# Gate silus placed behind the last exponential of the decays in a hybrid convolution and state-space layer

## The chip, the cores and the metric

The kernel runs on one core of a Trainium2 chip. The metric is the device time of one execution in microseconds. Before the change the median of three runs is 1958.61 us (1958.3 to 1961.29).

The engines are named as in the profile: PE is TensorE (matmuls), DVE is VectorE, ACT is ScalarE, POOL is GpSimd, SP is SyncE, which here only issues DMAs. Each engine takes its instructions in the order in which they stand in its own queue, and waits in that order.

## The reference

One layer mixes a convolution branch and a Mamba-2 (SSD) branch, and a gated MLP with a short convolution follows. 1024 positions, width 1024. What matters here is the SSD branch, in chunks of 128 positions, 4 groups of 8 heads:

```python
a_cs = jnp.cumsum(a, axis=-1)
seg = a_cs[..., :, None] - a_cs[..., None, :]
decay = jnp.where(causal, jnp.exp(jnp.where(causal, seg, 0.0)), 0.0)
cb = jnp.einsum("bclgn,bcsgn->bcgls", cc, bc)
y_diag = jnp.einsum("bcgrls,bcsgrp->bclgrp", cb[:, :, :, None] * decay, xs)
...
yg = (y.reshape(bsz, t, SSM_DIM) * jax.nn.silu(z.astype(jnp.float32)))
```

`decay` needs an exponential, and `silu(z)` is the gate with which the branch's output is multiplied. `z` is a part of the input projection `h @ w_in`.

## The kernel before

The sequence is done in two halves of 512 positions (`hh` 0 and 1), each by `mixers(hh, hT)`. Every fp32 matrix is split in a high and a low part and a product takes three matmuls (`mm3`, L183 to L185), so that a column block of 128 channels (`column`) costs PE 24 matmuls of 128x512. Its result lies in one of four PSUM banks (`acc`), which are used in turn: a bank comes free when another engine has read the result. `col_weights` loads a block's weights by DMA, ACT makes the high part (L149) and, in half 0, DVE the low part (L154).

`mixers` goes through four groups. For each one it makes the column blocks of B, C and four of x, with a convolution of four taps (`conv4`: u on ACT, L417 to L419, taps on DVE, L421, a silu on ACT, L431); then the four gate blocks (`z_gate`, a silu on ACT at L483 straight out of PSUM into `zs`); then two blocks for the long convolution (`glu`, with a sigmoid, L442); then the SSD itself (`ssd_group`); then the 31 taps of the long convolution (`conv31`, L466), on DVE at the lowest priority.

`ssd_group` runs over the group's four chunks. Per chunk: `ab` (the cumulated sums, spread over the partitions by a DMA from SP, L506); eight Relus into `m` (L519) and one exponential over `m` (L526); an exponential `ce` (L529), which POOL multiplies with C (L530); the masked product of `m` (L546) on DVE; matmuls with `m` and `ce` on PE (L551, L554); the state (L559 to L566); the gate product (L579). `m`, `ab` and `ce` have one buffer each, so that the Relus of a chunk wait until PE has used up the `m` of the chunk in front of it.

The order in which instructions stand on the engines is set by a scheduler of the build, which estimates times and goes by priorities. A manual dependency (`issue_after`) orders two instructions of the same engine without a wait. The scheduler lets the column blocks of one group run among the SSD chunks of the group in front of it: so the gate silus of group g stand on ACT among the Relus and exponentials of the last chunk of group g - 1. ACT holds one table of functions at a time; where a silu follows an exponential, or the other way round, the build puts an ACT_TABLE_LOAD between them.

Of the kernel before, what the change touches and what calls it, by code (L numbers as in the profile page):

```python
# [10 lines left out]
AF = mybir.ActivationFunctionType  # L11
# [39 lines left out]
CT_A, CT_G, CT_X, CT_B, CT_C, CT_GA, CT_GB, CT_Z = 0, 8, 16, 32, 36, 40, 48, 56  # L51
# [4 lines left out]
def kernel(  # L56
# [16 lines left out]
    V, A, G, TE, SY = nc.vector, nc.scalar, nc.gpsimd, nc.tensor, nc.sync  # L73
# [14 lines left out]
    def bank(which):  # L88
        n_ps[0] += 1
        pl, tag = (pacc, "acc") if which else (psm, "sm")  # L90
        return pl.tile([P, 512], F32, tag=tag, name=f"{tag}{n_ps[0]}")
# [17 lines left out]
        out=quads, in_=ident.rearrange("p (j h) -> p h j", j=4), axis=AX.X, op=ALU.add  # L109
# [29 lines left out]
    }  # L139
    y_scr = [dram.tile([8, P, HALF], F32, name=f"y_scr{i}") for i in range(2)]  # L140

    casts, los = [], []

    def weights(src, name, keep=None, kept=None):
        with tc.high_priority(offset=4000):
# [16 lines left out]
    def col_weights(hh, ct):  # L162
        scr = low_scr.get(ct)
        return weights(
            wcol[ct], f"c{hh}_{ct}", None if hh else scr, scr if hh else None
        )

    def issue_after(later, earlier):

        tc.add_manual_dep(  # L170
            later.ins,
            earlier.ins.name,
            mybir.DependencyInfo(mybir.DependencyClass.NoSync, mybir.DependencyReason.DATA),
            reason="issue order",
        )
# [11 lines left out]
    def project(ps, w, xs):  # L187
        for k in range(KD):
            mm3(
                ps,  # L190
                lambda i: w[:, i, k * P : (k + 1) * P],
                lambda i: xs[:, i, k, :],
                k == 0,
                k == KD - 1,
            )
# [63 lines left out]
    def ln_in_first():  # L259
        hT = big_tile("hT0")  # L260
        with pool("lnin0", side="right") as pl:
            xts, gb = [], []
            for t in range(4):
                with tc.high_priority(offset=6000 if t < 2 else 3500):
                    xt = pl.tile([P, D], F32, tag="x", bufs=4, name=f"x0_{t}")
                    SY.dma_start(xt, x[t * P : (t + 1) * P, :])
                    xts.append(xt)
                    if t == 0:
                        for i, n in enumerate(("in_g", "in_b")):
                            gb.append(pl.tile([P, D], F32, name=n))  # L270
                            SY.dma_start(gb[i], gin[i])
            SY.dma_start(pc[:, :PC_N], pcol)
            SY.dma_start(a_log, prow[RW_AL : RW_AL + HEADS].partition_broadcast(P))
            for t, xt in enumerate(xts):
                with tc.high_priority(offset=6000 if t < 2 else 3500):
                    mv, rs = ln_stats(pl, [xt], f"in0_{t}")
                    ln_apply(xt, mv, rs, 0, *gb)
                    G.dma_start(h_scr[0][t * P : (t + 1) * P, :], xt)
                    transpose_to(hT, xt, t, 0, KD)
        return hT  # L280
# [84 lines left out]
    def column(hh, hT, ct):  # L365
        ps = bank(1)
        project(ps, col_weights(hh, ct), hT)
        return ps
# [110 lines left out]
    def z_gate(pl, hh, hT, g):  # L479

        zs = pl.tile([P, 4, HALF], F32, tag="zs", bufs=2, name=f"zs{hh}_{g}")
        for i in range(4):
            A.activation(out=zs[:, i, :], in_=column(hh, hT, CT_Z + 4 * g + i), func=AF.Silu)  # L483
        return zs

    held = []
# [1 line left out]
    def ssd_group(pl, hh, g, xT, BT, CT, zs):  # L488
# [3 lines left out]
        def heads(t):  # L492
            return t.rearrange("p (h q) -> p h q", h=8)

        def per_head(t):
            return t.unsqueeze(2).to_broadcast([P, 8, HP])

        ssum = pl.tile([P, HALF], F32, tag="ssum", name=f"ssum{hh}_{g}")
        for c in range(4):
# [17 lines left out]
            m = pl.tile([P, 8, P], F32, tag="m", name=f"m{nm}")  # L517
            for h in range(8):
                A.activation(  # L519
                    out=m[:, h, :],  # L520
                    in_=ab[:, h, :],
                    func=AF.Relu,
                    scale=-1.0,
                    bias=acs[:, c, 8 * g + h : 8 * g + h + 1],
                )
            A.activation(out=m, in_=m, func=AF.Exp, scale=-1.0)  # L526
            if not first:
                ce = pl.tile([P, 8, P], F32, tag="ce", name=f"ce{nm}")
                A.activation(out=ce, in_=ab, func=AF.Exp)  # L529
# [1 line left out]
                    out=ce, in0=ce, in1=CT[:, cs].unsqueeze(1).to_broadcast([P, 8, P]), op=ALU.mult  # L531
# [5 lines left out]
                out=heads(xs), in0=heads(px), in1=per_head(dts[0][:, c, h8]), op=ALU.mult  # L537
            )
            if not last:
                xsd = pl.tile([P, HALF], F32, tag="xsd", name=f"xsd{nm}")  # L540
                V.tensor_tensor(
                    out=heads(xsd), in0=heads(px), in1=per_head(dts[1][:, c, h8]), op=ALU.mult
# [14 lines left out]
            if not last:  # L557
# [4 lines left out]
                else:  # L562
                    V.tensor_tensor(
                        out=heads(S), in0=heads(S), in1=per_head(edc[:, 1, c, h8]), op=ALU.mult
                    )
                    V.tensor_add(S, S, pn)  # L566
            for i in range(4):
                k = PC_SD + 4 * g + i
                skip = V.scalar_tensor_tensor(
                    out=xT[:, i, cs],  # L570
# [72 lines left out]
    def mixers(hh, hT):  # L643
        pre = first_columns(hh, hT, (CT_B, CT_C, CT_X))
        with pool(f"mixers{hh}") as pl:
            time_steps(pl, hh, pre[0])
            scaled = parts = None
            for g in range(GROUPS):
                BT = conv4(pl, hh, column(hh, hT, CT_B + g) if g else pre[1], 16 + g)
                CT = conv4(pl, hh, column(hh, hT, CT_C + g) if g else pre[2], 20 + g)  # L650
                xT = pl.tile([P, 4, HALF], F32, tag="x4", bufs=2, name=f"x4_{hh}_{g}")
                for i in range(4):
                    j = 4 * g + i
                    conv4(pl, hh, column(hh, hT, CT_X + j) if j else pre[3], j, xT[:, i, :])
                zs = z_gate(pl, hh, hT, g)
                vs = [(i, glu(pl, hh, hT, i)) for i in (2 * g, 2 * g + 1)]
                if g:
                    scaled()
                if g == 1:
                    yT = big_tile(f"yT{hh}_0")  # L660
                if g in (1, 2):
                    parts(yT)
                split_2 = parts
                scaled, parts = ssd_group(pl, hh, g, xT, BT, CT, zs)
                if g == 3:
                    ssm_out_first(pl, hh, yT)
                    yT = big_tile(f"yT{hh}_2")
                    split_2(yT)
                    gate_first(pl, hh, hT, range(3))
                    scaled()  # L670
                    parts(yT)
                with tc.high_priority(offset=-1500):
                    accs = conv31(pl, hh, vs)
            gate_first(pl, hh, hT, range(3, 8))
# [522 lines left out]
    hT = ln_in_first()  # L1197
    yT, accs = mixers(0, hT)
    mixT, hT = combine(0, hT, yT, accs)
# [129 lines left out]
```

## Time and profile before

| what | value |
|---|---|
| median of 3 runs | 1958.61 us |
| the profiled execution | 1960.26 us |
| its span, first to last instruction | 1958.4 us |
| mean granted TensorE clock | 0.997 |
| ACT_TABLE_LOADs at the lines of exponentials, L526 and L529 | 15 and 22 |
| ACT_TABLE_LOADs at the line of the gate silus, L483 | 11 |

All rows of a timeline start with the start and the duration in us, then engine, line, operation, output and inputs; in brackets stands the idle time of the engine just before, and what ended it. "x8" at the end means eight instructions in one row. A busy time per engine counts neither semaphores nor the issue of DMAs. The line of a helper stands for all who call it, such as L183 to L185 for every product.

### The profile page before, as it was taken

The numbers are of one execution on the slowest core, as the hardware profiler recorded it, in microseconds if no ns is written. First come the engines' busy times: TensorE is split into PE (matmuls) and PEld (weight loads), VectorE is DVE, ScalarE is ACT, GpSimd is POOL, SyncE is SP. The second block draws the span as 40 slices with busy tenths as digits, with TensorE's granted clock in tenths as the row PEclk, the third lists the DMA queues.
The fourth block names the chain that finished last, engine by engine and source line by source line (L and its number), as shares of the span: only waits on it lengthen the run. The fifth ranks groups of instructions, "written<-read, shape, count | busy, mean of one in ns | idle before, by whom it ended". The sixth has DMA issues, their size and how long they took to land.

```text
span 1958.4 us, 25837 instructions
## 1 busy us (share of the span) xinstructions
PE 1929.1 (99%) x9453; PEld 1574.9 (80%) x9453; DVE 1599.8 (82%) x2224; ACT 1081.2 (55%) x1615; POOL 218.9 (11%) x258
## 2 busy tenths in 40 slices
PE   9999999999999999999999999999999999989997
PEld 8888878788788788888878888888888888867886
DVE  7599999999786538898999546587788888879778
ACT  4676767653263266777765435365555555544432
POOL 0001010112210001111112140010000000121010
PEclk9999999999999999999999999999999999999999
DMA  7645555447355565556545644566455455588673
GB/s 270 224 166 205 174 202 185 159 171 245 116 188 212 198 214 175 205 181 208 176 159 168 216 145 134 188 237 230 163 167 189 166 188 178 198 301 276 195 230 127
DMA packets 127648, 378.36 MB, mean 193 GB/s; under 512 B 15104, under 2 KB 15648, under 8 KB 127520
## 3 DMA queue, kind: packets, MB, share of 16 engines
q1 hardware_dynamic: 107424, 318.48, 48.2%
q0 software_dynamic: 13760, 46.69, 6.9%
q10 hardware_dynamic: 6336, 11.54, 1.6%
q8 instruction: 74, 1.21, 0.3%
q14 instruction: 54, 0.44, 0.1%
HBM read 289.99 MB, written 86.65 MB: 192 GB/s over the span
## 4 chain that ended last, share of the span: by engine, by line
PE 60%; DVE 10%; DMA 3%; ACT 2%; issue 2%; DVEq 0%; SPq 0%; ACTq 0%
PE acc L185 13%; PE acc L184 13%; PE acc L183 13%; PE sm L184 6%; PE sm L185 6%; PE sm L183 6%; DVE c L466 4%; DMA dr<-wdown 1%; DVE x L421 1%; DMA st_wo<-wo 1%; DMA b_scr<-fo 1%; PE sm L551 1%; PE sm L554 0%; DVE m L546 0%; ACT m L519 0%
## 5 line engine op out<-in xcount | busy, mean ns | idle before, releaser
L183 PE MATMUL acc<-hT,w_c 128*128 128x512 f32 x1000 | 391.2, 391 | 0.0
L185 PE MATMUL acc<-hT,w_c 128*128 128x512 f32 x1000 | 391.1, 391 | 0.0
L184 PE MATMUL acc<-hT,w_c 128*128 128x512 f32 x1000 | 391.0, 391 | 0.0
L466 DVE SCALAR_TENSOR_TENSOR c<-v,pc,c 128x512 f32<-128x512 f32 x480 | 369.7, 798 | 7.3 <-ACT c L455 4.5
L183 PEld LDWEIGHTS acc<-hT,w_c 128*128 128x128 f32 x1000 | 187.8, 188 | 40.6 <-issue 1.9
L185 PEld LDWEIGHTS acc<-hT,w_c 128*128 128x128 f32 x1000 | 187.8, 188 | 40.0 <-issue 1.5
L184 PEld LDWEIGHTS acc<-hT,w_c 128*128 128x128 f32 x1000 | 187.8, 188 | 39.5 <-issue 1.1
L149 ACT CAST w_c<-st_c 128x1024 fp32r<-128x1024 f32 x128 | 133.9, 1046 | 127.6 <-PE acc L185 100.6
L530 POOL TENSOR_TENSOR ce<-ce,xbc 128x1024 f32<-128x1024 f32 x28 | 82.2, 2936 | 681.7 <-ACT ce L529 681.7
L1116 ACT CAST w_dn<-dr 128x1024 fp32r<-128x1024 f32 (+1 forms) x73 | 68.6, 944 | 88.3 <-DMA dr<-wdown 36.7
L183 PE MATMUL sm<-h1s,w_s 128*128 128x512 f32 x264 | 102.7, 389 | 0.0
L184 PE MATMUL sm<-h1s,w_s 128*128 128x512 f32 x264 | 102.7, 389 | 0.0
L185 PE MATMUL sm<-h1s,w_s 128*128 128x512 f32 x264 | 102.2, 389 | 0.0
L519 ACT ACTIVATE m<-ab,acs 128x128 f32<-128x128 f32 x256 | 78.3, 390 | 37.7 <-PE sm L551 36.6
L154 DVE TENSOR_TENSOR w_c<-st_c,w_c 128x1024 fp32r<-128x1024 f32 x64 | 79.4, 1243 | 22.3 <-ACT w_c L149 17.1
L1117 DVE TENSOR_TENSOR w_dn<-dr,w_dn 128x1024 fp32r<-128x1024 f32 (+1 forms) x73 | 78.9, 1092 | 6.1 <-ACT w_dn L1116 6.1
L421 DVE SCALAR_TENSOR_TENSOR x<-u,pc,x 128x512 f32<-128x512 f32 x96 | 78.8, 835 | 3.9 <-ACT x L419 3.8
L185 PE MATMUL acc<-h1b,w_ue 128*128 128x512 f32 x176 | 68.8, 394 | 0.3 <-DVE w_ue L154 0.3
L183 PE MATMUL acc<-h1b,w_ue 128*128 128x512 f32 x176 | 68.7, 390 | 0.0
L184 PE MATMUL acc<-h1b,w_ue 128*128 128x512 f32 x176 | 68.5, 389 | 0.0
L183 PE MATMUL sm<-h1b,w_s 128*128 128x512 f32 x176 | 68.5, 389 | 0.0
L184 PE MATMUL sm<-h1b,w_s 128*128 128x512 f32 x176 | 68.5, 389 | 0.0
(325 smaller groups left out, 4547.3 us busy)
## 6 DMA issues: line engine op xcount, KB each, us to landing
st_c<-wcol SPq DMA_DIRECT2D x128, 512.0 KB, 4.4
low_scr<-w_c SPq DMA_DIRECT2D x64, 512.0 KB, 2.9
w_c<-low_scr SPq DMA_DIRECT2D x64, 512.0 KB, 4.4
ab<-acs_scr SPq DMA_DIRECT2D x32, 512.0 KB, 4.1
dr<-wdown SPq DMA_DIRECT2D x55, 256.0 KB, 5.2
st_wo<-wo SPq DMA_DIRECT2D x24, 512.0 KB, 4.5
st_ue<-wup SPq DMA_DIRECT2D x22, 512.0 KB, 3.6
first_scr<-first ACTq DMA_DIRECT2D x44, 256.0 KB, 3.0
```

What stands on the lines that cost most here:

```text
L149: casts.append(A.copy(w[:, 0, :], st))
L154: V.tensor_tensor(out=w[:, 1, :], in0=st, in1=w[:, 0, :].bitcast(F32), op=ALU.subtract)
L183: TE.matmul(ps, wa(0), xa(0), start=start, stop=False, skip_group_check=more)
L184: TE.matmul(ps, wa(0), xa(1), start=False, stop=False, skip_group_check=more)
L185: TE.matmul(ps, wa(1), xa(0), start=False, stop=stop, skip_group_check=more)
L421: V.scalar_tensor_tensor(out=o, in0=u[:, k : k + HALF], scalar=pc[:, wc + k : wc + k + 1], in1=o, op0=ALU.mult, op1=ALU.add,)
L466: V.scalar_tensor_tensor(out=accs[i], in0=v[:, k : k + HALF], scalar=pc[:, wc + k : wc + k + 1], in1=accs[i], op0=ALU.mult, op1=ALU.add,)
L519: A.activation(out=m[:, h, :], in_=ab[:, h, :], func=AF.Relu, scale=-1.0, bias=acs[:, c, 8 * g + h : 8 * g + h + 1],)
L530: G.tensor_tensor(out=ce, in0=ce, in1=CT[:, cs].unsqueeze(1).to_broadcast([P, 8, P]), op=ALU.mult)
L551: TE.matmul(o, xs[:, h * HP : (h + 1) * HP], m[:, h, :], start=True, stop=first)
L1116: A.copy(w[:, 0, cs], src)
L1117: V.tensor_tensor(out=w[:, 1, cs], in0=src, in1=w[:, 0, cs].bitcast(F32), op=ALU.subtract)
```

## The change

The build is given an order: in `z_gate` the second, third and fourth silu of a group (i = 1, 2, 3) are placed on ACT behind the last exponential of `m` (`exps[-1]`) that has been written down by then, which is that of the last chunk of the group in front. Group 0 has none in front of it. The dependency is one of order only.

```diff
-    casts, los = [], []
+    casts, los, exps = [], [], []
...
         for i in range(4):
-            A.activation(out=zs[:, i, :], in_=column(hh, hT, CT_Z + 4 * g + i), func=AF.Silu)
+            silu = A.activation(
+                out=zs[:, i, :], in_=column(hh, hT, CT_Z + 4 * g + i), func=AF.Silu
+            )
+            if g and i:
+                issue_after(silu, exps[-1])
...
-            A.activation(out=m, in_=m, func=AF.Exp, scale=-1.0)
+            exps.append(A.activation(out=m, in_=m, func=AF.Exp, scale=-1.0))
```

In the rows of the build below, names end in the number of the group, then of the chunk where there is one, then a number of the build; from the changed lines on, line numbers are four higher (L519 is L523, L526 is L530, L529 is L533, L581 is L585). PE, DVE, POOL and SP have the same rows in the same order in both builds. ACT has 1421 rows before and 1417 now, and differs at four places: in both halves, around the last chunk of group 1 and of group 2.

ACT in half 1, at the last chunk of group 2 (m_2_3, ce_2_3) with the gates of group 3 (zs_3), before:

```order
L519 ACTIVATE m_2_3_8163<-ab_2_3_8154,acs 128x128 x8
L529 ACT_TABLE_LOAD
L529 ACTIVATE ce_2_3_8173<-ab_2_3_8154 128x1024
L149 CAST w_c_6_8633<-st_c_6_8631 128x1024
L483 ACT_TABLE_LOAD
L483 ACTIVATE zs_3_8504<-acc_8536 128x512
L526 ACT_TABLE_LOAD
L526 ACTIVATE m_2_3_8163<-m_2_3_8163 128x1024
L581 ACTIVATE sq_2_2_8150<-x_1_2_7540 128x512
L149 CAST w_c_14_8662<-st_c_14_8660 128x1024
L483 ACT_TABLE_LOAD
L483 ACTIVATE zs_3_8504<-acc_8567 128x512
```

and now:

```order
L523 ACTIVATE m_2_3_8163<-ab_2_3_8154,acs 128x128 x8
L533 ACT_TABLE_LOAD
L533 ACTIVATE ce_2_3_8173<-ab_2_3_8154 128x1024
L149 CAST w_c_6_8633<-st_c_6_8631 128x1024
L530 ACTIVATE m_2_3_8163<-m_2_3_8163 128x1024
L483 ACT_TABLE_LOAD
L483 ACTIVATE zs_3_8504<-acc_8536 128x512
L585 ACTIVATE sq_2_2_8150<-x_1_2_7540 128x512
L149 CAST w_c_14_8662<-st_c_14_8660 128x1024
L483 ACTIVATE zs_3_8504<-acc_8567 128x512
```

The exponential of `m` has moved ahead of one silu, and two of the table loads are gone. The place at the last chunk of group 1 in half 1 has the same two orders, with its own tiles.

ACT in half 0, at the last chunk of group 1 (m_1_3) with the gates of group 2 (zs_2), before:

```order
L483 ACTIVATE zs_2_2485<-acc_2518 128x512
L431 ACTIVATE x_0_2_2324<-x_0_2_2324,pc 128x512
L149 CAST w_c_12_2648<-st_c_12_2646 128x1024
L483 ACTIVATE zs_2_2485<-acc_2550 128x512
L519 ACTIVATE m_1_3_2124<-ab_1_3_2114,acs 128x128 x8
L529 ACT_TABLE_LOAD
L529 ACTIVATE ce_1_3_2134<-ab_1_3_2114 128x1024
L526 ACTIVATE m_1_3_2124<-m_1_3_2124 128x1024
L431 ACT_TABLE_LOAD
L431 ACTIVATE x_0_2_2324<-x_0_2_2324,pc 128x512
```

and now:

```order
L431 ACTIVATE x_0_2_2324<-x_0_2_2324,pc 128x512
L149 CAST w_c_12_2648<-st_c_12_2646 128x1024
L523 ACTIVATE m_1_3_2124<-ab_1_3_2114,acs 128x128 x8
L533 ACT_TABLE_LOAD
L533 ACTIVATE ce_1_3_2134<-ab_1_3_2114 128x1024
L530 ACTIVATE m_1_3_2124<-m_1_3_2124 128x1024
L483 ACT_TABLE_LOAD
L483 ACTIVATE zs_2_2485<-acc_2518 128x512
L483 ACTIVATE zs_2_2485<-acc_2550 128x512
L431 ACTIVATE x_0_2_2324<-x_0_2_2324,pc 128x512
```

Two silus have moved from ahead of the Relus to behind the exponential; the number of table loads is the same. The place at the last chunk of group 2 in half 0 differs in the same way, and there the first tap of a channel block (L455) now comes behind the two silus.

## The prediction

> **What bounds the kernel now.** I read the page first: engine shares, then the rows that explain a stall.
>
> ```profile
> span 1958.4 us, 25837 instructions
> ...
> PE 1929.1 (99%) x9453; PEld 1574.9 (80%) x9453; DVE 1599.8 (82%) x2224; ACT 1081.2 (55%) x1615; POOL 218.9 (11%) x258
> ```
>
> PE works in 1929.1 of 1958.4 us, so all that any change of order can save is 29.3 us of PE idle. The busy time by stretches (columns: stretch, its length, PE busy, ...) says where that idle lies: of the stretches of 20 us in which the four places of the change stand, one has a hole of size.
>
> ```profile
> 980.00:1000.00 20.00, 17.48 (x120) 14.14 (x116) 19.03 (x31) 15.53 (x23) 2.98 (x1) 1.00 0.46 156
> ...
> 1740.00:1760.00 20.00, 17.40 (x73) 13.08 (x72) 17.06 (x21) 7.36 (x7) 4.71 (x10) 1.00 0.95 337
> ```
>
> The first loses 2.5 us; the second, far behind the change, is quoted for a rival. The waits between 860 and 1000 us (total, times, longest) name what is waited for:
>
> ```profile
> PE sm L551 <- DVE m L546: 2.7, 2, 2.5
> DVE m L546 <- ACT m L526: 1.9, 2, 1.0
> ```
>
> PE waits for the masked decays of VectorE (L546), and VectorE twice, 1.0 us each, for the exponential (L526) of ScalarE. The change moves silus behind that exponential.
>
> **The change part by part.** The build moves instructions at four places only, all on ACT; at group 1 the silus stood behind the exponential already. I call half 0's places C (near 257 us, group 2's gates) and D (348 us, group 3's), half 1's A (897 us) and B (991 us).
>
> Place B, the timeline of all engines:
>
> ```profile
> 985.08 0.72 ACT L431 ACTIVATE x<-x,pc 128x512 f32<-128x512 f32 x1 [3.13 <-DVE x L421]
> 987.91 1.42 DVE L466 SCALAR_TENSOR_TENSOR c<-v,pc,c 128x512 f32<-128x512 f32 x2
> 990.42 1.03 ACT L149 CAST w_c<-st_c 128x1024 fp32r<-128x1024 f32 x1
> 990.60 2.98 POOL L530 TENSOR_TENSOR ce<-ce,xbc 128x1024 f32<-128x1024 f32 x1 [16.47 <-ACT ce L529]
> 991.23 3.57 DVE L466 SCALAR_TENSOR_TENSOR c<-v,pc,c 128x512 f32<-128x512 f32 x2
> 991.47 1.28 ACT L483 ACT_TABLE_LOAD   x1
> 992.77 0.60 ACT L483 ACTIVATE zs<-acc 128x512 f32<-128x512 f32 x1
> 993.38 1.28 ACT L526 ACT_TABLE_LOAD   x1
> 994.68 1.06 ACT L526 ACTIVATE m<-m 128x1024 f32<-128x1024 f32 x1
> 995.77 1.23 DVE L546 TENSOR_TENSOR m<-m,cbm 128x1024 f32<-128x1024 f32 x1 [0.97 <-ACT m L526]
> ...
> 994.01 0.39 PE L183 MATMUL acc<-hT,w_c 128*128 128x512 f32 x1
> 994.24 0.39 PE L184 MATMUL acc<-hT,w_c 128*128 128x512 f32 x1
> 997.14 0.44 PE L551 MATMUL sm<-m,xs 128*64 128x128 f32 x4 [2.52 <-DVE m L546]
> ```
>
> Before, ACT goes cast, table load, silu, table load, exponential. Now the exponential follows the cast: it starts at 990.42 + 1.03 = 991.45 in place of 994.68, which is 3.2 us earlier. Two table loads of 1.28 us go at this place (the one ahead of the exponential, and one ahead of a later silu), and two at A: 5.1 us of ACT work in all. At C and D the number of loads stays.
>
> PE does not get the 3.2 us. VectorE takes its instructions in order, and two conv taps (L466) stand in front of L546. They end at 991.23 + 3.57 = 994.80, so L546 starts at 994.80 in place of 995.77: **0.97 us** are won, which is just the idle time in its row. Why these taps take 3.57 us, when the two at 987.91 take 1.42, is seen in the POOL row: a GpSimd multiply runs from 990.60 to 993.58, and the pair ends 1.22 us behind it. The floor of 994.80 therefore moves only if POOL moves.
>
> The Trainium skill, "SBUF — State Buffer", section "Who interferes with whom", states that a DVE instruction with two SBUF inputs and a GpSimd instruction that reads SBUF exclude each other whole, and the rows agree (1.22 us behind POOL's end for two taps). Without such a lock the taps would end near 991.23 + 1.42 = 992.65, and by the exponential's earlier end the whole 2.52 us would go, for some 1956.1 us.
>
> Place A has the same pattern, but PE does not stand there:
>
> ```profile
> 897.39 1.28 ACT L483 ACT_TABLE_LOAD   x1
> 899.31 1.28 ACT L526 ACT_TABLE_LOAD   x1
> 900.60 1.06 ACT L526 ACTIVATE m<-m 128x1024 f32<-128x1024 f32 x1
> ...
> 901.69 1.22 DVE L546 TENSOR_TENSOR m<-m,cbm 128x1024 f32<-128x1024 f32 x1 [0.98 <-ACT m L526]
> ```
>
> VectorE wins 0.98 us here, which is worth nothing at once. It counts if it is still there at 985, where ACT's silu (the row at 985.08) waits for VectorE, and the Relus, the exponentials and the POOL multiply of place B come behind that silu. So I followed the 84 us between for a point that would swallow the lead:
>
> ```profile
> 919.96 0.22 ACT L443 COPY v<-v_halo 128x30 f32<-128x30 f32 x1 [5.81 <-DVE c L466]
> 923.07 0.69 DVE L444 TENSOR_TENSOR v<-acc,sig 128x512 f32<-128x512 f32 x1 [3.14 <-ACT sig L442]
> ...
> 939.42 2.45 ACT L519 ACTIVATE m<-ab,acs 128x128 f32<-128x128 f32 x8 [1.34 <-PE sm L551]
> 944.28 0.75 DVE L421 SCALAR_TENSOR_TENSOR xbc<-u,pc,xbc 128x512 f32<-128x512 f32 x1
> 944.34 3.56 POOL L530 TENSOR_TENSOR ce<-ce,xbc 128x1024 f32<-128x1024 f32 x1 [5.27 <-ACT ce L529]
> 944.94 0.69 DVE L563 TENSOR_TENSOR state<-state,edc 128x512 f32<-128x512 f32 x1
> 946.58 3.85 DVE L605 SCALAR_TENSOR_TENSOR x<-x,pc,rstd 128x512 f32<-128x512 f32 x4
> 964.96 0.72 ACT L431 ACTIVATE xbc<-xbc,pc 128x512 f32<-128x512 f32 x1 [2.81 <-DVE xbc L421]
> ```
>
> At 923.07 VectorE waits 3.14 us for ACT, but ACT itself waited for VectorE at 919.96, so both move together. The weak point is 944: the Relus at 939.42 wait for PE, which gains nothing before B, so POOL's multiply cannot start before 944.34. Its 3.56 us are long beside the 2.98 above, which looks like POOL held up by the two VectorE instructions at 944.28 and 944.94, to 945.54. With the lead these end near 944.6, POOL ends as much earlier, and the L605 behind it too. I take it that 0.95 us survive. Where POOL keeps its end at 947.90, nothing survives. At 964.96 ACT waits for VectorE again.
>
> If the lead arrives, place B starts 0.95 earlier as a whole, and L551 starts at 997.14 - 0.97 - 0.95 = 995.22. That leaves 0.6 us of the hole, since PE's last matmul ends at 994.24 + 0.39 = 994.63. **Sum at B: 1.9 us**, with bounds of 0 (the exponential is early and something else is late) and 2.5 (the whole hole).
>
> Places C and D add a wait that could bite: the silus free the PSUM banks of the column products, and now come behind Relus that wait for PE. Behind the moved silus on ACT are a conv silu, casts and the bank copies.
>
> ```profile
> 251.28 2.45 ACT L519 ACTIVATE m<-ab,acs 128x128 f32<-128x128 f32 x8
> 252.89 0.39 PE L516 MATMUL sm<-xbc,xbc 128*128 128x128 f32 x2
> 256.01 1.05 ACT L526 ACTIVATE m<-m 128x1024 f32<-128x1024 f32 x1
> 263.76 1.06 ACT L149 CAST w_c<-st_c 128x1024 fp32r<-128x1024 f32 x1 [2.25 <-PE acc L185]
> ...
> 344.25 0.39 PE L516 MATMUL sm<-xbc,xbc 128*128 128x128 f32 x2
> 347.47 1.06 ACT L526 ACTIVATE m<-m 128x1024 f32<-128x1024 f32 x1
> 350.32 0.82 ACT L455 ACTIVATE c<-v,pc 128x512 f32<-128x512 f32 x1 [1.80 <-DMA c_scr<-c]
> 353.66 0.74 DVE L466 SCALAR_TENSOR_TENSOR c<-v,pc,c 128x512 f32<-128x512 f32 x1
> ```
>
> C: the first moved silu ends at 256.01 + 1.05 + 1.28 + 0.60 = 259.0 (a load and a silu as at 991.47 and 992.77). The four banks go round, and the next product in its bank begins 22 + 24 matmuls behind 252.89 in PE's order, at 0.23 us each (from 994.01 to 994.24), so near 263.5. There are 4.5 us to spare. What follows on ACT is 1.2 us late, and the idle 2.25 us ahead of 263.76 takes that in, and the DMAs issued behind those casts have as long. D: the silu ends near 350.4, its bank is wanted near 344.25 + 10.6 = 354.8: 4.4 us to spare. The first tap of the next channel block (L455) starts at 351.0 in place of 350.32 and ends by 351.9, VectorE wants it at 353.66. Both places cost **nothing**; without that cover each us over costs one.
>
> The profiled execution is 1960.26 us, 1.86 around its span, and 1.65 above the median of 1958.61. 1960.26 - 1.9 = 1958.3; carried to the median: **1956.7**, a gain of 0.1%. A measurement of this kernel can tell about 0.2% (3.9 us) from no change.
>
> **The rivals.** (1) The lead from A is lost at POOL's multiply at 944: 0.97 us remain, 1957.6. For it speaks that the start of that multiply hangs on PE; against it its length of 3.56. (2) Nothing arrives: what PE gains at B it stands still for later, at 1740 for instance, where 2.6 us are idle at a DMA share of 0.95: 1958.6. Against it: buffers there come free by PE, so loads start earlier too. (3) ACT's saving counts in full: 4 x 1.28 = 5.1 us, 1953.5. It needs ACT to set the pace; at 55% busy, with waits of 5.81 and 3.13 us in the rows above, it does not.
>
> The Trainium skill, "ScalarE: Activation LUTs", section "What ACT_TABLE_LOAD costs", puts 1.38 us of drain behind each load, 2.66 us a switch, and advises to group calls by table set. By it four switches would be an estimated 10.6 us, or 1948.0. The trace shows no drain: the load at 993.38 ends at 994.66, the exponential starts at 994.68.
>
> (4) Slower: at C and D the Relus come late, the moved silus hold their banks, and PE stands still. It decides from 4.5 us of lateness on; with Relus 6.5 us late at both, PE loses 2 us twice: 1962.6. Against it: at 251.28 they start as PE lets them go, without idle time of their own.
>
> **How the numbers follow.** Forecast (1.9 us, the lead survives) 0.50; rival 1 0.20; rival 2 0.12; rival 3 0.04; rival 4 0.06; 0.08 for what I have not seen, half on each side. Over 0.2% faster is rival 3 and half the rest, rounded up: 0.09; slower is rival 4 and half the rest: 0.10; the others 0.81. The range takes in the whole hole at B (1956.1) and no gain (1958.6), each with about two microseconds for the spread of medians (the three runs before lie within 3.0): 1954.4 to 1961.0.
>
> **What would show it.** L526 should follow the cast at A and B without a table load; L546 should start behind its taps without the 0.97 us wait; PE's wait in front of L551 at B should be 0.6 us (1.5 if rival 1 holds). There should be four ACT_TABLE_LOADs less, and no new PE wait near 263 and 355. I am wrong if VectorE waits at B for something else, or if new PE holes show behind 1000 us.

## The result and the profile after

| | before | with the change |
|---|---|---|
| median of 22 runs each | 1961.16 us | 1958.06 us |
| lowest to highest | 1958.3 to 1967.26 us | 1954.4 to 1962.4 us |
| span of the profiled execution | 1958.4 us | 1955.3 us |

The ratio is 0.9981, with a 95% interval of 0.9975 to 0.9988: 3.7 us less, between 2.4 and 4.9; the medians alone differ by 3.1. The forecast was 1.9 us less. Its 1956.7 us were counted from 1958.61, the median of three runs; over 22 runs the same kernel has 1961.16, so the difference is what can be compared, not the time.

The page after, in the line of the engine shares: PE's work is the same to 0.4 us, ACT has four instructions and 5.8 us less.

```profile
span 1955.3 us, 25833 instructions
...
PE 1928.7 (99%) x9453; PEld 1574.1 (81%) x9453; DVE 1598.4 (82%) x2224; ACT 1075.4 (55%) x1611; POOL 213.9 (11%) x258
```

The stretch of 20 us in which place B stands lost 2.5 us of PE time before; now it loses 0.6:

```profile
980.00:1000.00 20.00, 19.40 (x120) 15.59 (x116) 19.93 (x33) 16.63 (x30) 3.00 (x1) 1.00 0.53 176
```

Place B after the change, in the timeline of all engines (line numbers are four higher: L530 is the exponential of `m`, L550 the masked product, L555 the matmuls with it):

```profile
988.95 1.03 ACT L149 CAST w_c<-st_c 128x1024 fp32r<-128x1024 f32 x1
989.12 3.00 POOL L534 TENSOR_TENSOR ce<-ce,xbc 128x1024 f32<-128x1024 f32 x1 [16.47 <-ACT ce L533]
989.77 3.56 DVE L466 SCALAR_TENSOR_TENSOR c<-v,pc,c 128x512 f32<-128x512 f32 x2
989.89 1.06 ACT L530 ACTIVATE m<-m 128x1024 f32<-128x1024 f32 x1
990.96 1.28 ACT L483 ACT_TABLE_LOAD   x1
992.25 0.60 ACT L483 ACTIVATE zs<-acc 128x512 f32<-128x512 f32 x1
993.25 1.21 DVE L550 TENSOR_TENSOR m<-m,cbm 128x1024 f32<-128x1024 f32 x1
...
994.61 0.44 PE L555 MATMUL sm<-m,xs 128*64 128x128 f32 x4 [0.60 <-DVE m L550]
```

The exponential follows the cast directly. It is done at 990.95, and the masked product still starts only at 993.25, as the two taps end: the product no longer waits for ACT, but for the taps in front of it on VectorE. PE waits 0.60 us in place of 2.52.

The weak point of the forecast was the GpSimd multiply near 944 us. This execution is 0.4 us ahead of the one before already at place A, which has to be taken off the times. Its rows after:

```profile
939.03 2.45 ACT L523 ACTIVATE m<-ab,acs 128x128 f32<-128x128 f32 x8 [2.40 <-PE sm L555]
943.49 0.69 DVE L567 TENSOR_TENSOR state<-state,edc 128x512 f32<-128x512 f32 x1
943.95 2.49 POOL L534 TENSOR_TENSOR ce<-ce,xbc 128x1024 f32<-128x1024 f32 x1 [5.72 <-ACT ce L533]
945.12 3.85 DVE L609 SCALAR_TENSOR_TENSOR x<-x,pc,rstd 128x512 f32<-128x512 f32 x4
```

It starts as before behind Relus that wait for PE (944.34 less 0.39), but takes 2.49 us in place of 3.56. The 1.07 us are those by which VectorE is earlier here (its update of `state` starts 944.94 - 943.49 = 1.45 us earlier, less the same 0.39): that the multiply no longer has to wait for VectorE is read from these rows.

### The profile page after: what moved, and what is told of

It reads as the page before. It is cut to its first block, busy times and chain, and to the rows that moved or that the text cites. A ratio compares the mean times of both kernels' runs of the same rounds, so it can differ in the third digit from the quotient of the medians.

```text
span 1955.3 us, 25833 instructions
## 1 busy us (share of the span) xinstructions
PE 1928.7 (99%) x9453; PEld 1574.1 (81%) x9453; DVE 1598.4 (82%) x2224; ACT 1075.4 (55%) x1611; POOL 213.9 (11%) x258
## 3 DMA queue, kind: packets, MB, share of 16 engines
q8 instruction: 74, 1.21, 0.3%
## 4 chain that ended last, share of the span: by engine, by line
PE 55%; DVE 13%; DMA 5%; issue 2%; ACT 1%; SPq 0%; DVEq 0%; POOL 0%; ACTq 0%; POOLq 0%
PE acc L185 12%; PE acc L183 12%; PE acc L184 12%; PE sm L184 5%; PE sm L185 5%; PE sm L183 5%; DVE c L466 4%; DMA dr<-wdown 2%; DVE w_dn L1121 1%; DMA dr<-b_scr 1%; DVE x L421 1%; DMA b_scr<-fo 1%; DVE rows L244 1%; PE sm L555 1%; DVE rows L247 1%
## 5 line engine op out<-in xcount | busy, mean ns | idle before, releaser
L534 POOL TENSOR_TENSOR ce<-ce,xbc 128x1024 f32<-128x1024 f32 x28 | 77.1, 2752 | 682.4 <-ACT ce L533 682.4
L523 ACT ACTIVATE m<-ab,acs 128x128 f32<-128x128 f32 x256 | 78.4, 390 | 41.2 <-PE sm L555 40.3
```

The costliest lines, as they stand in the source:

```text
L523: A.activation(out=m[:, h, :], in_=ab[:, h, :], func=AF.Relu, scale=-1.0, bias=acs[:, c, 8 * g + h : 8 * g + h + 1],)
L534: G.tensor_tensor(out=ce, in0=ce, in1=CT[:, cs].unsqueeze(1).to_broadcast([P, 8, P]), op=ALU.mult)
```

## The experiments

Start, middle and end of the program move by themselves from execution to execution. So I read each profile in four stretches, bounded by three rows: the first of the Relus at place A (near 891 us), the first matmul with `m` behind B's hole (L551 or its new number), and the first transposes of the MLP part (L869, 1269.61 us before).

| profile | start to A | A to B | B to L869 | L869 to end |
|---|---|---|---|---|
| before | 891.62 | 105.52 | 272.47 | 688.8 |
| before_again | 890.99 | 105.50 | 272.48 | 688.0 |
| before_third | 890.86 | 105.51 | 272.48 | 688.6 |
| half0_only | 892.45 | 105.50 | 272.48 | 690.3 |
| only_A | 890.58 | 104.42 | 272.48 | 694.0 |
| only_B | 888.41 | 104.43 | 272.50 | 690.3 |
| whole change | 891.24 | 103.37 | 272.50 | 688.2 |
| whole_again | 891.38 | 103.36 | 272.47 | 688.9 |
| whole_third | 889.59 | 103.39 | 272.47 | 689.0 |
| half1_only | 892.46 | 103.38 | 272.47 | 686.4 |
| multiply_on_DVE | 892.50 | 103.84 | 271.34 | 692.1 |
| taps_behind | 892.77 | 103.98 | 273.83 | 688.0 |

The middle two columns repeat to 0.03 us for the same order of instructions. In the last two rows PE's matmuls themselves stand in another order at B, so the two columns have to be added there.

**half1_only.** The order is given in half 1 alone.

```diff
-            if g and i:
+            if hh and g and i:
```

> The order is given in half 1 alone (places A and B); half 0 is as before. My theory (the gain is made at B, half 0 costs and gives nothing): the first L551 behind the 32 us of place B starts with an idle time of 0.6 us, as with the whole change, in place of 2.52; the stretch from the Relus of place A to that L551 is 103.4 us as with the whole change, in place of 105.5; the time is that of the whole change, ratio 0.998 to 0.999 to before. Rival (half 0 gives part of the 3.7 us): the stretch is still 103.4, but the ratio is nearer to 1 than with the whole change, by up to 0.0008, and PE's wait near 509 us is 4.2 us as before, not 3.6.

Measured: ratio 0.9983 (0.9974 to 0.9992), A to B 103.38 us, idle time before L551 0.60 us; PE's wait near 509 us was 4.0 us, against 4.2 and 3.6 in the profiles of before and of the whole change. Half 1 has the whole gain, as far as the ratios can tell.

**half0_only.** The order in half 0 alone (places C and D).

```diff
-            if g and i:
+            if not hh and g and i:
```

> The order is given in half 0 alone (places C and D), where ACT's table loads keep their number. My theory: no new PE wait near 263 and 355 us, idle time before L551 at B is 2.5 us as before, ratio 1.000 within 0.0007. Rival (half 0 gives part): ratio 0.999 or below, with PE's wait near 509 us at 3.6 us. Rival (the banks are held): new PE idle time near 263 or 355 us, ratio above 1.

Measured: ratio 0.9997 (0.9988 to 1.0005), A to B 105.50 us, idle time before L551 2.50 us, PE's wait near 509 us 4.4 us. Places C and D cost nothing and give nothing that can be seen, with an interval from 2.4 us less to 1.0 us more. The 3.6 us near 509 in the profile of the whole change was no effect of half 0: over all profiles this wait is 3.3 to 4.2 us with half 0 as before and 3.5 to 4.4 us with half 0 changed.

**only_A.** Place A alone.

```diff
-            if g and i:
+            if hh and g == 2 and i:
```

> Only place A has the order (half 1, gates of group 2): B keeps its silu and its two table loads between the cast and the exponential. If the 1 us that VectorE wins at A lives until B, everything at B comes 1.0 to 1.1 us earlier and the idle time before L551 falls from 2.52 to about 1.5 us, with VectorE's wait of 0.97 us in front of the masked product still there. If the lead is lost on the way (at the GpSimd multiply near 944 us), the idle time stays at 2.5 us. Ratio by the first: 0.9994.

Measured: ratio 0.9997 (0.9988 to 1.0005), which says nothing at this size. The profile does: the rows of place B in its timeline:

```profile
988.46 2.99 POOL L534 TENSOR_TENSOR ce<-ce,xbc 128x1024 f32<-128x1024 f32 x1 [16.46 <-ACT ce L533]
989.12 3.54 DVE L466 SCALAR_TENSOR_TENSOR c<-v,pc,c 128x512 f32<-128x512 f32 x2
992.54 1.06 ACT L530 ACTIVATE m<-m 128x1024 f32<-128x1024 f32 x1
993.63 1.23 DVE L550 TENSOR_TENSOR m<-m,cbm 128x1024 f32<-128x1024 f32 x1 [0.97 <-ACT m L530]
...
995.00 0.44 PE L555 MATMUL sm<-m,xs 128*64 128x128 f32 x4 [1.64 <-DVE m L550]
```

VectorE's wait of 0.97 us at B is still there, since B has its old order, and yet PE waits 1.64 in place of 2.52, and A to B is 1.10 us shorter. The lead won at A arrives at B 90 us later, whole. The wait alone shows only 0.88 of the 1.10 us, because PE itself comes to B earlier: before, it had a second, short wait for a masked product, one chunk ahead of B, which is gone here and is still 0.15 us in only_B. Its row before:

```profile
979.35 0.44 PE L551 MATMUL sm<-m,xs 128*64 128x128 f32 x4 [0.17 <-DVE m L546]
```

**only_B.** Place B alone.

```diff
-            if g and i:
+            if hh and g == 3 and i:
```

> Only place B has the order (half 1, gates of group 3). The masked product starts right behind its two taps, without the wait of 0.97 us, and the idle time before L551 is about 1.55 us; the taps still end some 1.2 us behind the GpSimd multiply. If VectorE's floor (the taps held up by GpSimd) is not what limits, the idle time falls to 0. VectorE's wait of 0.98 us at A is as before. Ratio 0.9994.

Measured: ratio 0.9994 (0.9985 to 1.0004), A to B 104.43 us, 1.09 us shorter. The timeline of VectorE and PE at B:

```profile
988.01 3.55 DVE L466 SCALAR_TENSOR_TENSOR c<-v,pc,c 128x512 f32<-128x512 f32 x2
991.49 1.21 DVE L550 TENSOR_TENSOR m<-m,cbm 128x1024 f32<-128x1024 f32 x1
...
992.84 0.44 PE L555 MATMUL sm<-m,xs 128*64 128x128 f32 x4 [1.47 <-DVE m L550]
```

The masked product starts right behind its taps and PE waits 1.47 us: the taps are the floor, not the exponential. A and B together: 1.10 + 1.09 = 2.19, against 2.15 for the whole change (105.52 - 103.37).

**multiply_on_DVE.** The whole change, and the GpSimd multiply at place B done by VectorE.

```diff
-                G.tensor_tensor(
+                (V if (hh, g, c) == (1, 2, 3) else G).tensor_tensor(
```

> The whole change, and the GpSimd multiply of place B (half 1, last chunk of group 2) is done by VectorE instead, between the two conv taps. PE has five column matmuls more in front of L551 here, so its idle time there is 0 either way; VectorE's rows tell. By my theory (the taps were held up by GpSimd) the two taps take 0.75 us each and the masked product starts about 2.5 us behind the start of the first tap (0.67 + 1.14 + 0.67), which is 1 us earlier than with the whole change (3.5 us) in spite of the added work. Rival (the taps are slow for another reason, such as a table load beside them): they still take 2.1 us more than two taps do, and the masked product starts over 4.5 us behind the first tap. Time by my theory: up to 0.6 us less than the whole change, ratio 0.998 to 0.9985 to before.

Measured: ratio 0.9981 (0.9972 to 0.9990). VectorE at B:

```profile
991.05 0.74 DVE L466 SCALAR_TENSOR_TENSOR c<-v,pc,c 128x512 f32<-128x512 f32 x1
991.17 1.05 ACT L530 ACTIVATE m<-m 128x1024 f32<-128x1024 f32 x1
991.72 1.21 DVE L534 TENSOR_TENSOR ce<-ce,xbc 128x1024 f32<-128x1024 f32 x1
992.24 1.28 ACT L483 ACT_TABLE_LOAD   x1
992.85 0.74 DVE L466 SCALAR_TENSOR_TENSOR c<-v,pc,c 128x512 f32<-128x512 f32 x1
993.51 1.21 DVE L550 TENSOR_TENSOR m<-m,cbm 128x1024 f32<-128x1024 f32 x1
```

Without the GpSimd multiply beside them the taps take 0.74 us each, with ACT's table load still running beside the second. The masked product starts 2.46 us behind the first tap, in place of 3.48 (989.77 to 993.25), with one instruction more ahead of it. So GpSimd is what stretches the taps. From A to L869 this kernel takes 375.18 us, the whole change 375.87: the last 0.6 us of the hole are gone too. That does not show the exclusion by itself, since PE has five more column matmuls in front of L551 here, which fill the hole. Its ratio cannot be told from that of the whole change.

**taps_behind.** The whole change, and the two taps in front of the masked product at A and B are placed behind it.

```diff
+                if (hh, i, k) in behind:
+                    issue_after(tap, masked[behind[hh, i, k]])
...
-            V.tensor_tensor(out=m, in0=m, in1=cbm.unsqueeze(1).to_broadcast([P, 8, P]), op=ALU.mult)
+            masked[hh, g, c] = V.tensor_tensor(
+                out=m, in0=m, in1=cbm.unsqueeze(1).to_broadcast([P, 8, P]), op=ALU.mult
+            )
```

`behind` holds tap 26 of the group's first channel block and tap 15 of its second, in half 1, for groups 1 and 2, each with the last chunk of its group.

> The whole change, and at A and B the two taps in front of the masked product go behind it. The build then also puts L551 six column matmuls earlier on PE (1.4 us), and two table loads come back behind the exponential. By my theory (an exclusion of VectorE and GpSimd, whichever instruction stands there) the masked product now takes the delay itself: its end lies about 1.1 us behind the end of the GpSimd multiply, near 2.9 to 3.4 us behind that multiply's start, and PE waits about 0.7 us in front of L551; the time is that of the whole change within 0.5 us. Rival (only the taps were slow): the masked product starts as the exponential ends and takes 1.2 us, PE does not wait at B, and the time is 0.6 us less.

Measured: ratio 0.9995 (0.9987 to 1.0004). Place B in its timeline, where L556 is the masked product:

```profile
992.54 2.98 POOL L540 TENSOR_TENSOR ce<-ce,xbc 128x1024 f32<-128x1024 f32 x1 [16.46 <-ACT ce L539]
993.30 1.05 ACT L536 ACTIVATE m<-m 128x1024 f32<-128x1024 f32 x1
994.39 2.22 DVE L556 TENSOR_TENSOR m<-m,cbm 128x1024 f32<-128x1024 f32 x1 [1.12 <-ACT m L536]
...
996.75 0.44 PE L563 MATMUL sm<-m,xs 128*64 128x128 f32 x4 [1.54 <-DVE m L556]
```

Now the masked product takes the delay: 2.22 us in place of 1.21, with its end 1.09 us behind that of the multiply (995.52), so that nearly all of its own 1.21 us come after the multiply. That fits the exclusion. The time was missed: PE waits 1.54 us, not 0.7, and A to L869 is 1.9 us longer than with the whole change (377.81 to 375.87), where I had expected 0.5 at most. Part of it lies ahead of B: the table load in front of `ce` at B starts 97.3 us behind A here, 95.5 with the whole change and 96.5 before. So the lead from A is gone in this kernel. It is gone early. A silu and two table loads (913.53 and 915.44) now stand ahead of the next chunk's exponential. Behind them VectorE waits 1.96 us for ACT at 918.35, where the whole change has no such wait, and the copy of `v_halo` on ACT (L443 before) starts 29.1 us behind A, against 27.3 with the whole change and 28.3 before. That these two loads cost the lead is read from the rows; no run tests it alone.

**before_again, whole_again, before_third.** One more profile each, for the spread of the untouched stretches.

> The kernel before, for another profile of it: how far do the stretches that the change does not touch move by themselves? If the measured gain over the 2.1 us of places A and B is scatter, the start up to place A (888.4 to 892.5 us so far) and the part behind L551 of B (958.9 to 966.5 us) are anywhere within some microseconds in both kernels. If the change also shortens the part behind B, this is 961 us or more here and below 961 us with the change. The stretch from A to B is 105.5 us.

> The whole change, for another profile of it. Stretch from the Relus of A to L551 of B 103.4 us, idle time there 0.6 us. Behind L551 of B: anywhere between 958.9 and 966.5 us if the rest is scatter, below 961 us if the change shortens that part too.

> The kernel before, a third profile for the spread of the parts that the change does not touch: start to place A 888 to 893 us, behind L551 of place B 959 to 967 us, the stretch between 105.5 us.

Measured: the rows of the table. Behind L869 the kernel before takes 688.0 to 688.8 us in three profiles, the whole change 688.2 to 689.0 in three. There is no sign that the change shortens the end.

**whole_third.** The whole change timed a second time, beside other runs of the kernel before.

> The whole change, timed a second time apart from the first, against runs of the kernel before that are taken beside it. If the 1.6 us by which the first ratio (0.9981) went beyond the 2.1 us of places A and B were scatter, this ratio lies nearer to 0.9989, and its interval takes that value in. If the change also saves 1.6 us elsewhere, it lies near 0.9981 again. In the profile: stretch from A to B 103.4 us, idle time in front of L551 0.6 us.

Measured: ratio 0.9983 (0.9972 to 0.9993), A to B 103.39 us, idle time 0.61 us. The interval takes in 0.9989, the ratio of the 2.15 us, and 0.9981 as well. It does not decide.

## Why the prediction held

- **The mechanism and its place.** PE waited at B for the masked product, the product for the exponential, and the silu between cast and exponential was the cause. PE's wait was forecast to fall from 2.52 to 0.6 us; it is 0.60. That it fits so well is in part luck. The two leads were taken to be 0.97 + 0.95 = 1.92 us and are 2.15, and PE comes to B 0.23 us earlier (102.77 us behind A in place of 103.00), so the two differences cancel. Most of the 0.23 is the wait of 0.17 us at 979.35, which stands in the prediction's total of 2.7 us but not in its sum.
- **The floor of the taps.** That only about 1 us of the exponential's 3.2 would count at B, because two taps held up by GpSimd stand in front of the product, is borne out by only_B (1.09 us) and multiply_on_DVE. Without GpSimd beside them the taps take 0.74 us each. The Trainium skill states such an exclusion in "SBUF — State Buffer", section "Who interferes with whom", and these rows agree with it.
- **The size of that term.** I took the start of the product to be 994.80, the end of the taps' row: 0.97 us. Rows on VectorE overlap: with the change the taps' row ends at 989.77 + 3.56 = 993.33, and the product's row starts at 993.25. The end of the taps' row is here 0.08 us later than the start of the product, and that is most of the difference to the 1.09 us of only_B.
- **The lead from A.** I took 0.95 us to survive; only_A shows 1.10. At A itself the lead is already 1.06 us and not 0.98 (the product starts 9.01 us behind the first Relu, in place of 10.07). The multiply near 944 us gave way as forecast: 2.49 us in place of 3.56, and 2.48 in only_A, while in only_B, without the lead, it takes 3.56 as before. Rival 1 falls.
- **Places C and D.** Nothing was forecast and half0_only shows none. PE has no wait between 240 and 400 us in the profile of the whole change; rival 4 falls.
- **Given back later?** B to L869 is 272.47 to 272.50 us in all ten profiles with PE's old order at B, so what B wins is still there 272 us later; rival 2 falls as far as that. Behind L869 the spread is larger than the gain.
- **ACT's saving in full (rival 3).** Four table loads went, 5.1 us by their rows; the stretch from A to L869 has become 2.12 us shorter (377.99 to 375.87), so it does not count in full. Of a drain behind a load, as the Trainium skill has it in "ScalarE: Activation LUTs", section "What ACT_TABLE_LOAD costs", the rows after show none either: the load at 990.96 ends at 992.24, the silu starts at 992.25.
- **What stays open.** The sum was forecast at 1.9 us, and the steps as measured make 2.1. The first timing says 3.7 (2.4 to 4.9), which leaves both just outside its interval; the second says 3.3 (1.4 to 5.5), and half1_only, with the same two places, 3.3 (1.6 to 5.1). All three lie above 2.1; the spans of the three profiles of each kernel differ by 2.3 us on the mean (1957.6 to 1955.3). The profiles show no place for the other 1.2 to 1.6 us: half 0 shows no effect, and the end and the start lie within the spread. Whether this is scatter or a small effect of the change that single profiles do not catch, the runs do not tell. So the mechanism at A and B is shown, and the size of the whole gain is not.

## What to carry to other kernels

An instruction made earlier gains only up to the next thing that its reader stands behind: look at what is queued in front of the reader on its own engine before the whole lead is counted. A lead on an engine that PE does not wait for at that moment is not worthless: follow it along the rows to the next place where PE does wait, and check every point where another engine, free of the lead, could set the pace. Where a change is smaller than the scatter of whole runs, compare stretches between two rows of the profile that carry the effect.

## What the runs showed that I had not expected

The same stretch of the program repeats to 0.03 us in the middle, while the start up to A varies from 888.4 to 892.8 us and the part behind L869 from 686.4 to 694.0 us. In these profiles all of the scatter that hides an effect of 2 us in the medians lies there.

The exclusion between VectorE and GpSimd works in both directions and hands a lead on: VectorE's being 1.07 us earlier shortened the multiply from 3.56 to 2.49 us, although that started no earlier in relation to the Relus ahead of it.
